# Expert tokens past 128 as plain float32 blocks of 32 over four column quarters, gate-weighted results added to the residual rows in DRAM

## The chip, the cores and the metric

The kernel runs on one core of one Trainium2 chip. The metric is the device time of one execution in microseconds (us). Before the change three runs took 3171.59, 3177.5 and 3178.11 us, so the median is 3177.5 us. One more execution, of 3167.94 us, was recorded by the hardware profiler; every row below is from that one.

## The reference, cut to what matters

A block takes 2048 tokens of width 1024. A token mixer (not touched, but for the order of one loop) makes a residual `x`. A router then picks two of 32 experts for each token, with a weight each, and the experts' results are added to the residual:

```
f = modulate(rms_norm(x, norm_ffn_w), m[3], m[4])            # [2048, 1024]
g = softmax(f @ rg_w + rg_b);  top group, its probability p
e = (f @ re_w + re_b) of that group's 8 experts;  top 2
weight = p * softmax(top 2)                                   # 2 per token
for each of the 4096 assignments (token t, expert k):
    out = (silu(f[t] @ w1[k]) * (f[t] @ w3[k])) @ w2[k]       # 1024 -> 512 -> 1024
y[t] = sum over its two assignments of weight * out
x = x + m[5] * y
return rms_norm(x, final_norm_w)
```

All is float32. On the inputs used, 15 of the 32 experts get more than 128 assignments, 4 of these more than 160, and none more than 192.

## The kernel before, in words

**Three stages matter.** (1) The project and route stage makes `x1` and `f` for 16 tiles of 128 tokens, stores them in DRAM (`X1`, `FR`), computes 36 router logits a token (`logits`, line 678, then a transpose back, `placed`) and from them a table of row numbers for every expert. (2) The expert stage is a loop over 32 experts. (3) The tail reads the experts' results back from `YB` in DRAM, two rows a token, multiplies them by the weights (ScalarE, line 1046), adds them (lines 1048 to 1051), multiplies by `m5` (line 1054), adds the residual (line 1055), and normalises (lines 1057, 1186, 1187, 1062), tile by tile.

**Precision.** A float32 product is done as three fast products (`mm3`, lines 1356 to 1358) of a rounded part `hi` and a remainder `lo`. ScalarE makes `hi` of a 128x1024 block of weights (line 1212), VectorE or GpSimd makes `lo` (line 1213). Twelve such blocks of 512 KB make one expert.

**One expert.** GpSimd gathers 128 rows of `FR` by an indirect DMA (line 848, tile `xg128`), and, when the expert has more than 128 rows, up to 64 more (`xg64`). TensorE transposes them (line 865). `up` makes 2x512 columns and `down` 1024. The *main* rows take 72 products of 128x512 columns, 48 up and 24 down. The *rest* rows sit behind a branch (`tc.If(big > 128)`, line 873): their `hi` and `lo` are laid side by side as 128 columns, so two products per weight block do (line 880): 32 up and 16 down, 48 for each expert that has a rest. A scatter by GpSimd (line 917) writes the results to the assignment's row of `YB`.

**Order.** Every engine has one queue and works it in order. The code is written with one expert's `down` after the next expert's `up`, a scheduler then fixes the order of each queue, and pools of buffers (`mraw` 9, `mhi` and `mlo` 15 each) decide how far the loads of weights, on SyncE's queue, run ahead. The gather of an expert waits until the transposes of the expert before it have freed `xg128`. A branch costs each engine that takes part in it a compare and a jump, also where it isn't taken.

**In the mixer**, `d_states` (line 314) multiplies with 64 rows of the array at a time; `g` is the outer loop, the chunk `c`, whose parity picks the lower or the upper 64 rows, the inner one. Elsewhere there (lines 429, 434) a product uses 64 columns of the array and the heads take the two column halves in turn.

Of the kernel before, what the change touches and what calls it, by code (L numbers as in the profile page):

```python
# [181 lines left out]
def ssm(G, tc, dtr, XR, ZT, XC, XB, cumD, ecumD, elD, SBd, YT):  # L182
# [4 lines left out]
    with tc.tile_pool(reuse_waits="tile", name="sst", bufs=1) as st:  # L187
# [86 lines left out]
        with tc.tile_pool(reuse_waits="tile", name="sw", bufs=1) as wp, tc.tile_pool(reuse_waits="tile", name="ssp", bufs=2) as sp:  # L274
# [292 lines left out]
RAW, PARTS = 9, 15  # L567
AHEAD = 6
# [3 lines left out]
def ffn(tc, G, A, out, bcast, rsqrt, split, mm3, MT, MR, X1, FR, YB, mid):  # L572
# [7 lines left out]
    wt = [rp.tile([128, N], F32, name=f"wt{k}") for k in range(2)]  # L580
# [5 lines left out]
    asg = rp.tile([128, NBK], I32, name="asg")  # L586
    idx = rp.tile([128, NBK], I32, name="idx")
    ovt = rp.tile([128, 2 * OVB + 1], I32, name="ovt")
    ovf = rp.tile([128, OVB], F32, name="ovf")

    def assign(dst_a, dst_r, v, t):
# [3 lines left out]
        nc.vector.tensor_copy(dst_a, v)  # L595
        nc.vector.tensor_scalar(t, v, float(T), float(-T), op0=OP.is_ge, op1=OP.mult)
        return nc.vector.tensor_add(dst_r, v, t)
# [4 lines left out]
    with tc.tile_pool(reuse_waits="tile", name="wo", bufs=1, side="right") as wop, \  # L602
# [19 lines left out]
        rb = wop.tile([36, 1], F32, name="rb")  # L622
        nc.sync.dma_start(rb, A["rb"])
# [20 lines left out]
        def project(i, *between):  # L644
# [13 lines left out]
            nc.sync.dma_start(X1[i], x1)  # L658
# [4 lines left out]
        def turned(i, x1, f, ss_, lg):  # L663
# [8 lines left out]
            nc.sync.dma_start(FR[i * 128:(i + 1) * 128], f)  # L672
            return fT, lg

        def logits(fT, lg):
            pl = psum("sc")
            for k in range(8):
                nc.tensor.matmul(pl[0:36, 0:128], rw[:, k], fT[:, k], start=k == 0, stop=k == 7)
            lt = tp.tile([36, 128], F32, name="lt", bufs=2)
            nc.vector.tensor_scalar(lt, pl[0:36, 0:128], rb, None, op0=OP.add)  # L680
            return lt, lg

        def placed(lt, lg):
            pl = psum("sc")
            nc.tensor.transpose(pl[:, 0:36], lt, G.ident[0:36, 0:36])
            nc.vector.tensor_copy(lg, pl[:, 0:36])

        def route(p0, i0, M, lg):
# [77 lines left out]
            nc.vector.tensor_mul(wt[0][:, i0:i0 + M], pg, v1)  # L766
            nc.vector.tensor_mul(wt[1][:, i0:i0 + M], wt[0][:, i0:i0 + M], v2)
# [7 lines left out]
        for p, i in enumerate(order):  # L775
# [6 lines left out]
            def second(p=p):  # L782
                tiles[p] = logits(*tiles[p])
# [3 lines left out]
            at.setdefault(2 * p + 4, []).insert(0, lambda p=p: placed(*tiles[p]))  # L787
            if last:
                at[2 * p + 4].append(lambda g=(p0, i0, M, lg): route(*g))
            tiles[p] = i, *project(i, lambda: do(2 * p), lambda: do(2 * p + 1))  # L790
        for h in range(2 * N, 2 * N + 3):
# [4 lines left out]
        listed = assign(asg, idx, tab.rearrange("p s e -> p (s e)"), at)  # L796
# [11 lines left out]
    def unit(src, q=nc.sync, eng=nc.vector):  # L808
# [5 lines left out]
        return hi, lo  # L814

    class InTurn:

        def __init__(self, src):
            self.src, self.at, self.parts = src, None, None

        def __getitem__(self, u):
            if u != self.at:
                raw = ovp.tile([128, 1024], F32, name="oraw")
                nc.sync.dma_start(raw, self.src(u))
                hi = wp.tile([128, 1024], F32R, name="ohi", tag="xq")
                lo = wr.tile([128, 1024], F32R, name="olo", tag="xg64")
                split(raw, hi, lo)
                self.at, self.parts = u, (hi, lo)
# [3 lines left out]
    hf = [psum(f"hf{i}") for i in range(2)]  # L832
    for p in hf:
        nc.vector.memset(p, 0.0)

    xgs = [wr.tile([128, D], F32, name=f"xg{r}") for r in (128, 64)]
    for x in xgs:
        nc.gpsimd.memset(x, 0.0)
    xgs[1] = xgs[1][0:64]


    ENGINES = [mybir.EngineType.PE, mybir.EngineType.Pool]
    outs = []

    def gather(idx_ap, half, guard):
        xg = xgs[half]
        with guard():
            nc.gpsimd.indirect_dma_start(out=xg, out_offset=None, in_=FR,  # L848
                                         in_offset=bass.IndirectOffsetOnAxis(ap=idx_ap, axis=0),
                                         bounds_check=T - 1, oob_is_err=False)  # L850
        return xg

    def parts(src, n, half, name):

        r = 64 if half else 128
        if half:
            q = wp.tile([128, n, 128], F32R, name=name + "q")
            hi, lo = q[:, :, 0:64], q[:, :, 64:128]
        else:
            hi, lo = (wp.tile([128, n, 128], F32R, name=name + c) for c in "hl")  # L860
        for c in range(0, n, 512 // r):
# [4 lines left out]
            v = pt[:, :m * r].rearrange("p (k t) -> p k t", t=r)  # L866
            nc.scalar.copy(hi[:, c:c + m], v)
            nc.vector.tensor_sub(lo[:, c:c + m], v, hi[:, c:c + m].bitcast(F32))
        return [q] if half else [hi, lo]

    def products(ps, x, ws, n, guard):

        with guard():
            for p, w in zip(ps, ws):
                if len(x) == 2:
                    mm3(p, lambda k: (x[0][:, k], x[1][:, k]), w, range(n))
                else:
                    for k in range(n):
                        for i, wk in enumerate(w(k)):
                            nc.tensor.matmul(p, x[0][:, k], wk, start=k + i == 0, stop=k == n - 1 and i == 1)  # L880

    def whole(dst, p):

        nc.scalar.copy(dst, p[64:128])
        nc.vector.tensor_add(dst, dst, p[0:64])  # L885

    def up(x, w1, w3, guard):
        half = len(x) == 1
        pa = hf if half else [psum("mm"), psum("mm")]
        wv = lambda w: lambda k: tuple(t[:, (k % 2) * 512:(k % 2) * 512 + 512] for t in w[k // 2])  # L890
        products(pa, x, [wv(w1), wv(w3)], 8, guard)
        h = wp.tile([64 if half else 128, FF], F32, name=f"mh{int(half)}")
        if half:
            g = wp.tile([64, FF], F32, name="mg")
            whole(h, pa[0])
            whole(g, pa[1])
            nc.scalar.activation(h, h, AF.Silu)
            nc.vector.tensor_mul(h, h, g)
        else:
            nc.scalar.activation(h, pa[0], AF.Silu)  # L900
            nc.vector.tensor_mul(h, h, pa[1])
        return h

    def down(h, w2, guard, dst):
        half = len(h) == 1
        y = wp.tile([128, D], F32, name=f"my{int(half)}")[0:64 if half else 128]
        py = hf if half else [psum("sc"), psum("sc")]
        wv = lambda w, o: lambda k: tuple(t[:, o:o + 512] for t in w[k])
        products(py, h, [wv(w, 512 * c) for c, w in enumerate(w2)], 4, guard)
        if half:  # L910
            whole(y[:, 0:512], py[0])
            whole(y[:, 512:1024], py[1])
        else:
            nc.scalar.copy(y[:, 0:512], py[0])
            nc.vector.tensor_copy(y[:, 512:1024], py[1])
        with (guard if half else nullcontext)():
            d = nc.gpsimd.indirect_dma_start(out=YB, out_offset=bass.IndirectOffsetOnAxis(ap=dst, axis=0), in_=y,
                                             in_offset=None, bounds_check=2 * T - 1, oob_is_err=False)
        for o in outs:
            tc.declare_no_dep(d.ins, o.ins, reason="rows of other assignments")  # L920
        outs.append(d)

    def fetch(e_, b, guard):
        s = b * NE + e_
        return parts(gather(idx[0:64 if b else 128, s:s + 1], b, guard), 8, b, "x")
# [7 lines left out]
    def beyond():  # L933
# [5 lines left out]
        le = ovp.tile([128, OVB, 32], BF, name="le")  # L939
# [22 lines left out]


    x = [fetch(0, 0, nullcontext), fetch(0, 1, nullcontext)]
# [3 lines left out]
    big = nc.values_load(cnti[0:1, 0:1], engines=ENGINES, min_val=0, max_val=CAP)  # L968
    nguard = lambda big=big: tc.If(big > 128)
    for e_ in range(NE + 1):  # L970
        if e_ < NE:
            guard = nguard
            if e_ + 1 < NE:
                big = nc.values_load(cnti[0:1, e_ + 1:e_ + 2], engines=ENGINES, min_val=0, max_val=CAP)
                nguard = lambda big=big: tc.If(big > 128)
            h = [up(x[0], *w13, nullcontext), None]
            q = nc.sync if e_ else nc.gpsimd
        if last:
            t1 = parts(last[1], 4, 1, "h")
        if e_ < NE:  # L980
            h[1] = up(x[1], *w13, guard)
            if e_ + 1 < NE:
                x[0] = fetch(e_ + 1, 0, nullcontext)
                w13 = in_weights(e_ + 1, q)
            w2 = [unit(A["e2"][e_][:, u], q, eng=nc.gpsimd if u % 2 else nc.vector) for u in range(4)]
        if last:
            down(last[0], [last[2]] * 2, nullcontext, asg[:, e_ - 1:e_])
            down(t1, [last[2]] * 2, last[3], asg[0:64, NE + e_ - 1:NE + e_])
        if e_ < NE:
            last = parts(h[0], 4, 0, "h"), h[1], w2, guard  # L990
            if e_ + 1 < NE:
                x[1] = fetch(e_ + 1, 1, nguard)
# [4 lines left out]
    m5, fn, *e = [rp.tile([128, D], F32, name="mraw") for _ in range(RAW)]  # L997
# [582 lines left out]
```

## Time and profile before

| what | us |
|---|---|
| median of three runs | 3177.5 |
| the profiled execution | 3167.94 |
| its span | 3166.2 |
| expert stage, from 2246 to 3049 | 803 |
| tail, from the last product on TensorE at 3049 to the end | 117 |

Over the whole span TensorE (PE) is busy 2876.7 us (91%), VectorE (DVE) 1893.4 us (60%), ScalarE (ACT) 1243.8 us (39%) and GpSimd (POOL) 853.5 us (27%). HBM was read for 501.47 MB and written for 129.27 MB. TensorE's granted clock is a mean of 0.956 of its full level. A busy share is to be read by stage: in the expert stage TensorE hardly pauses, in the tail it does nothing.

### The profile page before, as it was taken

How to read it: one execution, taken by the hardware profiler on the slowest of the kernel's cores; microseconds unless marked ns; L12 is line 12 of the kernel's file. 1: busy time of each engine (PE TensorE's matmuls, PEld its weight loads, DVE VectorE, ACT ScalarE, POOL GpSimd, SP SyncE). 2: the span in 40 equal slices, each digit the busy share in tenths (PEclk: the TensorE clock that was granted, in tenths of full speed). 3: DMA queues.
4: the chain of work that ended last, by engine and by line, in shares of the span. 5: the costliest groups of instructions: out<-in, count | busy, mean ns of one | idle time of the engine just before them, and what ended most of it. 6: DMA issues, size and time to landing. Idle time of an engine off the chain costs nothing. (4 is left out here: it accounts for less than half of the span.)

```text
span 3166.2 us, 40956 instructions
## 1 busy us (share of the span) xinstructions
PE 2876.7 (91%) x14805; PEld 2291.8 (72%) x14805; DVE 1893.4 (60%) x2957; ACT 1243.8 (39%) x1754; POOL 853.5 (27%) x589
## 2 busy tenths in 40 slices
PE   7998999999877999899999999999699999999950
PEld 4887887777655677677777777877577887778740
DVE  4524125878775587333334334566888767786758
ACT  5411132322345032232113122222677667675744
POOL 3300010000014021013334333000446445444445
PEclk8999999999978899999999999999799999999975
DMA  7635244423128486765336335432788878887884
GB/s 303 233 122 194 86 159 155 140 84 106 51 82 272 123 225 208 244 233 199 130 120 216 126 120 163 143 133 107 276 310 308 283 271 322 299 302 271 283 327 172
DMA packets 241878, 625.50 MB, mean 198 GB/s; under 512 B 27832, under 2 KB 75608, under 8 KB 237944
## 3 DMA queue, kind: packets, MB, share of 16 engines
q1 hardware_dynamic: 208784, 513.34, 47.0%
q0 software_dynamic: 32880, 109.38, 10.2%
q8 instruction: 126, 2.06, 0.3%
q14 instruction: 88, 0.72, 0.1%
HBM read 501.47 MB, written 129.27 MB: 199 GB/s over the span
## 5 line engine op out<-in xcount | busy, mean ns | idle before, releaser
L1212 ACT CAST mhi<-mraw 128x1024 fp32r<-128x1024 f32 x384 | 387.3, 1051 | 12.8 <-DMA mraw<-e 12.4
L1213 DVE TENSOR_TENSOR mlo<-mraw,mhi 128x1024 fp32r<-128x1024 f32 x318 | 378.2, 1242 | 2.8 <-ACT mhi L1212 2.2
L1356 PE MATMUL ps_mm<-hb1h,wlo 128*128 128x512 f32 x800 | 320.6, 401 | 3.1 <-DVE wlo L1213 3.1
L1507 ACT ACTIVATE ev<-ps_mm 128x512 f32<-128x512 f32 x128 | 76.3, 598 | 617.4 <-PE ps_mm L1358 508.6
L1358 PE MATMUL ps_mm<-hb1h,whi 128*128 128x512 f32 x800 | 318.7, 398 | 0.0
L1357 PE MATMUL ps_mm<-hb1l,whi 128*128 128x512 f32 x800 | 318.3, 398 | 0.0
L1213 DVE TENSOR_TENSOR wlo<-wraw,whi 128x1024 fp32r<-128x1024 f32 x164 | 217.9, 1337 | 149.2 <-ACT whi L1212 149.0
L1356 PE MATMUL ps_mm<-hb0h,wlo 128*128 128x512 f32 x672 | 270.1, 402 | 16.5 <-DVE wlo L1213 12.9
L1357 PE MATMUL ps_mm<-hb0l,whi 128*128 128x512 f32 x672 | 270.1, 402 | 0.0
L1358 PE MATMUL ps_mm<-hb0h,whi 128*128 128x512 f32 x672 | 268.6, 400 | 0.0
L1557 POOL TENSOR_TENSOR macc<-macc,ev 128x512 f32<-128x512 f32 x96 | 167.0, 1740 | 306.8 <-DVE ev L1556 303.8
L1213 POOL TENSOR_TENSOR mlo<-mraw,mhi 128x1024 fp32r<-128x1024 f32 x66 | 212.9, 3241 | 133.9 <-ACT mhi L1212 124.2
L1212 ACT CAST whi<-wraw 128x1024 fp32r<-128x1024 f32 x176 | 182.1, 1045 | 154.4 <-PE ps_mm L1358 65.8
L1556 DVE TENSOR_TENSOR ev<-ev,ps_tr 128x512 f32<-128x512 f32 x96 | 65.7, 686 | 248.5 <-PE ps_tr L1358 244.8
L1356 PE MATMUL ps_mm<-mhi,xl 128*128 128x512 f32 x512 | 204.7, 400 | 0.1
L1358 PE MATMUL ps_mm<-mhi,xh 128*128 128x512 f32 x512 | 200.9, 392 | 0.3
L848 POOL DMA_INDIRECT xg<-d_FR,idx x48 | 129.4, 2696 | 264.8 <-PE ps_tr L865 196.7
L1357 PE MATMUL ps_mm<-mlo,xh 128*128 128x512 f32 x512 | 200.5, 392 | 0.3
L1356 PEld LDWEIGHTS ps_mm<-hb1h,wlo 128*128 128x128 f32 x800 | 151.7, 190 | 38.0 <-DVE wlo L1213 3.5
L1358 PEld LDWEIGHTS ps_mm<-hb1h,whi 128*128 128x128 f32 x800 | 151.6, 190 | 34.3 <-issue 2.8
L1357 PEld LDWEIGHTS ps_mm<-hb1l,whi 128*128 128x128 f32 x800 | 151.8, 190 | 31.9 <-issue 1.6
L1356 PEld LDWEIGHTS ps_mm<-hb0h,wlo 128*128 128x128 f32 x672 | 128.1, 191 | 46.5 <-DVE wlo L1213 14.9
(605 smaller groups left out, 6486.0 us busy)
## 6 DMA issues: line engine op xcount, KB each, us to landing
mraw<-e SPq DMA_DIRECT2D x372, 512.0 KB
wraw<-wg SPq DMA_DIRECT2D x80, 512.0 KB
wraw<-wt SPq DMA_DIRECT2D x40, 512.0 KB
aw<-adaw SPq DMA_DIRECT2D x64, 256.0 KB
d_GS<-ev SPq DMA_DIRECT2D x64, 256.0 KB
ev<-d_GS POOLq DMA_DIRECT2D x64, 256.0 KB, 4.6
yk<-d_YB SPq DMA_DIRECT2D x32, 512.0 KB
wraw<-wg POOLq DMA_DIRECT2D x24, 512.0 KB, 4.2
```

The lines of the kernel that those rows point to most:

```text
L848: nc.gpsimd.indirect_dma_start(out=xg, out_offset=None, in_=FR, in_offset=bass.IndirectOffsetOnAxis(ap=idx_ap, axis=0), bounds_check=T - 1 ...
L1212: nc.scalar.copy(hi, raw)
L1213: eng.tensor_sub(lo, raw, hi.bitcast(F32))
L1356: nc.tensor.matmul(ps, wl, xh, start=start and n == 0, stop=False)
L1357: nc.tensor.matmul(ps, wh, xl, start=False, stop=False)
L1358: nc.tensor.matmul(ps, wh, xh, start=False, stop=stop and n == len(ks) - 1)
L1507: nc.scalar.activation(g, ps, AF.Sigmoid)
L1556: nc.vector.tensor_mul(g, g, ps)
L1557: nc.gpsimd.tensor_add(acc, acc, g)
```

## The change

- **Rest rows.** They are no longer split. The transposed rows stay plain float32 (`plain`, tile `xq`), 32 at a time are the stationary operand, and the raw weights `mraw` are the moving operand, 256 columns a product. `quarters` puts four such products side by side, one for each quarter of 32 columns of the array. A block of 32 rows is behind its own branch: block 0 if the expert has more than 128 rows, block 1 if it has more than 160. A block is 32 products up and 16 down. With these inputs there are 15 + 4 = 19 blocks.
- **Weights at the gate.** `FR` gets a 1025th column with the assignment's weight and is stored twice, once for each of a token's two assignments. The gather brings the weight along, and it is multiplied in where `silu` meets the other half (lines 904 and 944); `m5` is multiplied in behind `down` (lines 921 and 952).
- **Results.** The scatter (line 908) adds to the rows of `X1` in DRAM; unused rows of a block go to 256 spare rows. Scatters to the same rows are ordered one after the other: the rest of an expert waits until its predecessor's main scatter has landed.
- **Tail.** It reads only `X1`, and normalises.
- **Buffers.** `mraw` 9 to 16, `mhi` and `mlo` 15 to 12 each. Raw blocks are held until the rest products have read them.
- **Router and mixer.** The logits are made with tokens on the rows (36 columns moving) and need no transpose back. In `d_states` the chunk is the outer loop.

```diff
-                for g, c in product(range(2), cs):
+                for c, g in product(cs, range(2)):
...
-RAW, PARTS = 9, 15
+RAW, PARTS = 16, 12
...
-            nc.sync.dma_start(FR[i * 128:(i + 1) * 128], f)
+            for k in range(2):
+                nc.sync.dma_start(FR[k * T + i * 128:k * T + (i + 1) * 128, 0:D], f)
...
-                nc.tensor.matmul(pl[0:36, 0:128], rw[:, k], fT[:, k], start=k == 0, stop=k == 7)
+                nc.tensor.matmul(pl[:, 0:36], fT[:, k], rw[:, k], start=k == 0, stop=k == 7)
...
+            for k in range(2):
+                nc.sync.dma_start(FR[k * T:k * T + T].rearrange("(i p) w -> p i w", p=128)[:, i0:i0 + M, D:D + 1],
+                                  wt[:, i0:i0 + M, k:k + 1])
...
+    def added(y, dst, out, no_dep=()):
+        d = nc.gpsimd.indirect_dma_start(out=out, out_offset=bass.IndirectOffsetOnAxis(ap=dst, axis=0), in_=y,
+                                         in_offset=None, compute_op=OP.add)
...
+    def quarters(p, n, guard, x, ws):
+
+        for j in range(2):
+            with guard(j):
+                for k, g in product(range(n), range(4)):
+                    nc.tensor.matmul(p[g * 32:g * 32 + 32, j * 256:j * 256 + 256], x(k, j), ws(k, g),
+                                     start=k == 0, stop=k == n - 1)
+
+    def up_rest(xw, w1, w3, guard):
+
+        w = [w1, w3]
+        quarters(hu, 8, guard, lambda k, j: xw[0][:, k, j * 32:j * 32 + 32],
+                 lambda k, g: w[g // 2][k // 2][2][:, (k % 2) * 512 + (g % 2) * 256:][:, 0:256])
...
+    def down_rest(h, w2, guard, e_):
+
+        quarters(hd, 4, guard, lambda k, j: h[:, j * 2 + k % 2, (k // 2) * 32:(k // 2) * 32 + 32],
+                 lambda k, g: w2[k][2][:, g * 256:g * 256 + 256])
+        y = wp.tile([128, 2, 256], F32, name="my1")
+        nc.vector.tensor_mul(y, hd.rearrange("p (j n) -> p j n", j=2), m5x.unsqueeze(1).to_broadcast([128, 2, 256]))
+        d = []
+        for j in range(2):
+            with guard(j):
+                d.append(added(y[:, j], sct4[:, e_, j:j + 1], X1.rearrange("r (g n) -> (r g) n", g=4), d))
+        return d
...
-    R = [(*rows(i), i) for i in range(AHEAD)]
-    for i in range(19):
-        if i + AHEAD < 16:
-            R.append((*rows(i + AHEAD), i + AHEAD))
-        if i < 16:
-            scaled(*R[i])
-        if 2 <= i < 18:
-            R[i - 2] += added(*R[i - 2]),
-        if i >= 3:
-            normed(*R[i - 3])
+    for i, t in enumerate(x1s):
+        nc.sync.dma_start(t, X1[i * 128:(i + 1) * 128])
+    for i, t in enumerate(x1s):
+        sq = wr.tile([128, D], F32, name="yk", tag=("mhi", "mlo")[i % 2], bufs=PARTS)
+        ss_ = wp.tile([128, 2], F32, name="ss3", bufs=4)
+        nc.scalar.activation(sq, t, AF.Square, accum_out=ss_[:, 0:1])
+        rsqrt(ss_[:, 1:2], ss_[:, 0:1], D, 1)
+        nc.vector.scalar_tensor_tensor(t, t, ss_[:, 1:2], fn, op0=OP.mult, op1=OP.mult)
+        nc.sync.dma_start(out[0][i * 128:(i + 1) * 128], t)
```

GpSimd's queue over one expert in the middle of the loop, before: `xg` is the gathers' tile, `mlo` the remainder of two weight blocks, `d_YB` the results in DRAM; L916 and L847 are the branches for the rest.

```order
541 L848 DMA xg_16987<-d_FR,idx 128x1024
...
545 L847 COMPARE_AND_BRANCH
546 L848 DMA xg_16988<-d_FR,idx 64x1024
...
550 L1213 TENSOR_TENSOR mlo<-mraw,mhi 128x1024 x2
551 L917 DMA d_YB<-my_21849,asg 4096x1024
552 L916 COMPARE_AND_BRANCH
553 L917 DMA d_YB<-my_21881,asg 4096x1024
...
559 L848 DMA xg_16987<-d_FR,idx 128x1024
```

The same after: `d_X_97` are the residual rows, `sct` and `sct4` the row numbers, and L955 the branches for the two rest blocks.

```order
654 L850 DMA xg_16950<-d_FR,idx 128x1025
...
657 L850 DMA xg_16951<-d_FR,idx 64x1025
...
665 L908 DMA d_X_97<-my_21968,sct 2304x1024
666 L1215 TENSOR_TENSOR mlo<-mraw,mhi 128x1024
...
671 L1215 TENSOR_TENSOR mlo<-mraw,mhi 128x1024
672 L955 COMPARE_AND_BRANCH
673 L908 DMA d_X_97<-my_22056,sct_17006 9216x256
...
677 L955 COMPARE_AND_BRANCH
678 L908 DMA d_X_97<-my_22056,sct_17006 9216x256
...
682 L850 DMA xg_16950<-d_FR,idx 128x1025
```

The main scatter now stands ahead of the two splits, the rest scatters behind them, and each gather stands behind the rest scatters, as it stood behind the scatters before.

TensorE's queue before, at the start of one expert's rest products: `xq` holds the rest rows, L873 is the branch.

```order
8675 L1358 MATMUL ps_mm<-mhi,xh 128x512
8676 L1356 MATMUL ps_mm<-mhi,xl 128x512
8677 L873 COMPARE_AND_BRANCH
8678 L880 MATMUL ps_hf_16983<-mhi,xq 128x512
8679 L880 MATMUL ps_hf_16983<-mlo,xq 128x512
```

After, the two blocks of another expert in the middle of the loop, each behind its own branch, L928.

```order
10016 L1360 MATMUL ps_mm<-mhi,xh 128x512
10017 L1358 MATMUL ps_mm<-mhi,xl 128x512
10018 L928 COMPARE_AND_BRANCH
10019 L930 MATMUL ps_hf_16946<-mraw,xq 32x256 x32
10020 L928 UNCONDITIONAL_BRANCH x2
10021 L928 COMPARE_AND_BRANCH
10022 L930 MATMUL ps_hf_16946<-mraw,xq 32x256 x32
10023 L928 UNCONDITIONAL_BRANCH x2
10024 L1359 MATMUL ps_mm<-mlo,xh 128x512
```

The rest products stay among the main products of the same expert; there are two branches where there was one.

VectorE's queue at the end of the tail, before: `ss` is one tile's sum of squares, `mraw` holds residual rows and `m5`, `yk` the results read back.

```order
2558 L1054 TENSOR_TENSOR yk_26833<-yk_26833,mraw 128x1024
2559 L1062 SCALAR_TENSOR_TENSOR mraw<-mraw,ss_26927 128x1024
2560 L1055 TENSOR_TENSOR mraw<-mraw,yk_26833 128x1024
2561 L1054 TENSOR_TENSOR yk_26849<-yk_26849,mraw 128x1024
2562 L1186 TENSOR_SCALAR ss_26935<-ss_26935 128x1
2563 L1055 TENSOR_TENSOR mraw<-mraw,yk_26849 128x1024
2564 L1062 SCALAR_TENSOR_TENSOR mraw<-mraw,ss_26935 128x1024
```

After:

```order
2489 L1189 TENSOR_SCALAR ss_28202<-ss_28202 128x1
2490 L1077 SCALAR_TENSOR_TENSOR mraw<-mraw,ss_28202 128x1024
2491 L1189 TENSOR_SCALAR ss_28209<-ss_28209 128x1
2492 L1077 SCALAR_TENSOR_TENSOR mraw<-mraw,ss_28209 128x1024
2493 L1189 TENSOR_SCALAR ss_28216<-ss_28216 128x1
```

Two instructions a tile are left, and each tile's pair is finished before the next one's begins.

## Rows read from the trace of the kernel before

**Rows 1.** Busy time by engine, a stretch of the expert stage, and the project stage

```profile
core 0: us, PE busy (x) PEld busy (x) DVE busy (x) ACT busy (x) POOL busy (x), PEclk, DMA share, GB/s
2340.00:2440.00 100.00, 98.42 (x477) 77.93 (x475) 85.47 (x104) 76.03 (x103) 61.84 (x22) 1.00 0.90 326
...
1905.00:2225.00 320.00, 312.63 (x1560) 247.78 (x1559) 188.58 (x488) 80.87 (x149) 40.27 (x40) 0.99 0.40 138
```

**Rows 2.** TensorE's timeline inside one rest: start, duration, line, tiles

```profile
2573.62 0.39 PE L880 MATMUL ps_hf<-mlo,xq 128*128 128x512 f32 x1
...
2576.79 0.40 PE L880 MATMUL ps_hf<-mlo,xq 128*128 128x512 f32 x1
```

**Rows 3.** The rest products alone over the expert stage, columns as far as ACT

```profile
2246.00:3049.00 803.00, 169.03 (x720) 134.94 (x720) 81.28 (x126) 71.65 (x126) 0.99 0.84 297
```

**Rows 4.** Timeline of plain float32 products, 256 moving columns, whole array

```profile
19.56 3.62 PE L1253 MATMUL ps_mm<-ha1h,s 128*2 128x256 f32 x16
23.11 0.28 PE L1261 MATMUL ps_sc<-c_kid,mr 2*128 2x2 f32 x2
```

**Rows 5.** Timeline of products by halves of the array, in the mixer

```profile
1107.44 0.64 PE L434 MATMUL ps_tr<-ec,Sf 128*64 128x64 f32 x16
1108.01 0.66 PE L319 MATMUL ps_sc<-xw,xb 64*64 64x128 f32 x8
1108.60 0.66 PE L429 MATMUL ps_tr<-PT,xb 128*64 128x128 f32 x8
```

**Rows 6.** Weight loads of line 434 there: duration in ns, minimum, median, maximum

```profile
L434 PEld LDWEIGHTS ps_tr<-ec,Sf x16: 137/138/138, 1107.3 to 1107.8; 128*64 128x64 f32 x16
```

**Rows 7.** Line 873, the rest's branch, in the expert stage

```profile
L873 PEldq COMPARE_BRANCH  x90: 65/169/357, 2304.4 to 3040.4; - x90
```

**Rows 8.** Gathers in the expert stage, and what their issue waited for

```profile
  PE ps_tr L865: 193.5, 35
...
DMA to landing us min/median/max: 4.2/8.1/12.9
```

**Rows 9.** Scatters in the expert stage

```profile
DMA to landing us min/median/max: 3.3/3.5/3.7
```

**Rows 10.** The tail, windows: its middle, its end, and its first loads

```profile
3063.00:3158.00 95.00, 0.00 (x0) 0.00 (x0) 86.77 (x72) 49.88 (x63) 54.67 (x32) 0.50 0.63 242
3158.00:3167.00 9.00, 0.00 (x0) 0.00 (x0) 0.00 (x0) 0.00 (x0) 0.00 (x0) 0.50 0.15 59
3060.00:3090.00 30.00, 0.00 (x0) 0.00 (x0) 23.64 (x18) 19.36 (x22) 17.45 (x9) 0.50 1.03 412
```

**Rows 11.** Chain of waits into the tail and at its end: start, duration

```profile
3052.67 3.73 DMA d_YB<-my,asg
...
3058.23 5.18 DMA yk<-d_YB
...
3152.45 0.17 DVE ss L1186
...
3152.75 1.41 POOL ss L1187
3154.18 1.28 DVE mraw L1062
```

**Rows 12.** Around the last product, and a tile's sum of squares, timeline

```profile
3048.79 0.39 PE L1358 MATMUL ps_sc<-mhi,hh 128*128 128x512 f32 x1
...
3069.80 1.06 ACT L1057 ACTIVATE yk<-xk 128x1024 f32<-128x1024 f32 x1 [3.92 <-DVE xk L1055]
```

**Rows 13.** Timeline of one tile's router logits

```profile
2000.73 1.94 PE L678 MATMUL ps_sc<-hb0l,rw 128*36 128x128 f32 x16
2002.60 0.50 PE L1356 MATMUL ps_mm<-y00h,wlo 128*128 128x512 f32 x1
```

**Rows 14.** Products of line 319 and of the logits, whole run

```profile
L319 PE MATMUL ps_sc<-xw,xb x280: 269/269/473, 956.0 to 1225.9; 64*64 64x128 f32 x140
...
L678 PE MATMUL ps_sc<-hb0l,rw x256: 272/273/421, 2000.7 to 2222.9; 128*36 128x128 f32 x128
```

More of the change, by code (lines that the diff above doesn't have):

```diff
@@ L849, in gather, with turned_into @@
                                          in_offset=bass.IndirectOffsetOnAxis(ap=idx_ap, axis=0),
-                                         bounds_check=T - 1, oob_is_err=False)
+                                         bounds_check=2 * T - 1, oob_is_err=False)
         return xg
[L853 to L860, printed above, removed]
+    def turned_into(put, src, r, n, w=128):
         for c in range(0, n, 512 // r):
@@ L865, in parts @@
                 nc.tensor.transpose(pt[:, k * r:(k + 1) * r], src[:, (c + k) * 128:(c + k + 1) * 128], G.ident[:r, :r])
[L866 to L901, printed above, removed]
-        return h
@@ L904, in down @@
[L904 to L921, printed above, removed]
@@ L923, in fetch, with parts, put @@
-    def fetch(e_, b, guard):
-        s = b * NE + e_
-        return parts(gather(idx[0:64 if b else 128, s:s + 1], b, guard), 8, b, "x")
+            put(slice(c, c + m), pt[:, :m * r].rearrange("p (k t) -> p k t", t=r))
+    def parts(src, n, name):
+        hi, lo = (wp.tile([128, n, 128], F32R, name=name + c) for c in "hl")
+        def put(c, v):
+            nc.scalar.copy(hi[:, c], v)
+            nc.vector.tensor_sub(lo[:, c], v, hi[:, c].bitcast(F32))
+        turned_into(put, src, 128, n)
+        return hi, lo
@@ new lines, in plain, with turn, turn_rest @@
+    def plain(src, n, name):
+        t = wp.tile([128, n, 64], F32, name=name)
+        turned_into(lambda c, v: nc.scalar.copy(t[:, c], v), src, 64, n)
+        return t
+    def turn(xg):
+        p = parts(xg, 8, "x")
+        w = wp.tile([128, 1], F32, name="w0", bufs=2)
+        nc.scalar.copy(w, xg[:, D:D + 1])
+        return p, w
+    def turn_rest(xg):
+        p = plain(xg, 8, "xq")
+        w = wp.tile([64, 2], F32, name="w1", bufs=2)
+        for j, h in product(range(2), range(2)):
+            nc.scalar.copy(w[h * 32:h * 32 + 32, j:j + 1], xg[j * 32:j * 32 + 32, D:D + 1])
+        return p, w
@@ new lines, in down @@
+    def down(h, w2, dst, rest=()):
+        y = wp.tile([128, D], F32, name="my0")
+        py = [psum("sc"), psum("sc")]
+        for c, (p, ws) in enumerate(zip(py, w2)):
+            o = slice(512 * c, 512 * c + 512)
+            mm3(p, lambda k: (h[0][:, k], h[1][:, k]), lambda k: tuple(t[:, o] for t in ws[k][:2]), range(4))
+            nc.vector.tensor_mul(y[:, o], p, m5[:, o])
+        added(y, dst, X1, rest)
+    def quarters(p, n, guard, x, ws):
[4 more added lines that the diff above has]
+                                     start=k == 0, stop=k == n - 1)
@@ L961, in beyond, with fetch @@
         nc.vector.scalar_tensor_tensor(ovf, bj, 128.0, ej, op0=OP.mult, op1=OP.add)
-    x = [fetch(0, 0, nullcontext), fetch(0, 1, nullcontext)]
+    def fetch(e_, guard):
+        xs = gather(idx[:, e_:e_ + 1], 0, nullcontext), gather(idx[0:64, NE + e_:NE + e_ + 1], 1, guard)
+        return lambda: (turn(xs[0]), turn_rest(xs[1]))
+    x = fetch(0, lambda: nullcontext())()
+    sct4 = wr.tile([128, NE, 2], I32, name="sct4")
+    for g, j in product(range(4), range(2)):
+        nc.gpsimd.tensor_scalar(sct4[g * 32:g * 32 + 32, :, j], sct[j * 32:j * 32 + 32, NE:], 4.0, float(g), op0=OP.mult, op1=OP.add)
     with tc.issue_after(listed.ins):
@@ L973, in ffn @@
             if e_ + 1 < NE:
-                big = nc.values_load(cnti[0:1, e_ + 1:e_ + 2], engines=ENGINES, min_val=0, max_val=CAP)
-                nguard = lambda big=big: tc.If(big > 128)
-            h = [up(x[0], *w13, nullcontext), None]
+                nguard = over(load(e_ + 1))
+            up_rest(x[1], *w13, guard)
+            h1 = gate_rest(x[1])
+            h = up(x[0], *w13)
+            t1 = plain(h1, 4, "hq")
             q = nc.sync if e_ else nc.gpsimd
+            if e_ + 1 < NE:
+                x = fetch(e_ + 1, lambda: nguard(0))()
+                w13 = in_weights(e_ + 1, q)
@@ L989, in ffn @@
[L989 to L992, printed above, removed]
+            rest = down_rest(t1, w2, guard, e_)
+            last = parts(h, 4, "h"), w2, rest
             if e_ == 4:
                 beyond()
-    m5, fn, *e = [rp.tile([128, D], F32, name="mraw") for _ in range(RAW)]
-    x1s = [wr.tile([128, D], F32, name="xk", tag=("mhi", "mlo")[i % 2], bufs=PARTS) for i in range(16 - len(e))] + e
@@ L1006, in ffn @@
+    otiles = x1s.pop(), *(wr.tile([128, 1024], F32R, name="o" + n, tag=n, bufs=PARTS) for n in ("mhi", "mlo"))
     with tc.issue_after(fetched.ins):
@@ L1053, in added @@
-    def added(y0, y1, x1, i):
-        nc.vector.tensor_mul(y0, y0, m5)
-        nc.vector.tensor_add(x1, x1, y0)
+        w1, w3 = (InTurn(lambda u, n=n: f2(n, u), otiles) for n in ("e1", "e3"))
+        w2 = [InTurn(lambda u: dy("e2")[:, u], otiles) for _ in range(2)]
+        h = up(turn(gather(ix, 0, nullcontext)), w1, w3)
+        down(parts(h, 4, "h"), w2, ixs)
+    for i, t in enumerate(x1s):
+        nc.sync.dma_start(t, X1[i * 128:(i + 1) * 128])
+    for i, t in enumerate(x1s):
+        sq = wr.tile([128, D], F32, name="yk", tag=("mhi", "mlo")[i % 2], bufs=PARTS)
```

152 lines of the change are left out of this document (68 added, 84 removed).

## Prediction

> **What bounds the kernel now.** I read the busy time by stretch first. In the expert stage TensorE works 98.42 of 100 us at a granted clock of 1.00, the upper of its two levels, while VectorE has 85, ScalarE 76 and GpSimd 62, and the DMA engines are at a share of 0.90 [rows 1]. The reader is to see that every other engine has room there, the transfers least. So the 803 us of this stage are a sum of TensorE's instructions, and the rest products are 169.03 us of them by busy time (720 records, 15 experts with 48 products each) [rows 3]. The project stage is TensorE's too, 312.63 of 320 us [rows 1]. Then the tail: from the last product at 3048.79 [rows 12] to the end of the span, 117 us, TensorE has nothing, and VectorE is busy 86.77 of the 95 us in the middle [rows 10]. The chain of waits shows how the tail starts (a scatter lands, 3.73, then the first load, 5.18) and ends (sum of squares, GpSimd's power, VectorE's multiply) [rows 11].
>
> **Rest products removed.** Two records of a rest 14 apart start 3.17 us apart, so one product costs 0.2264 us [rows 2], and 720 cost 163.0 us.
>
> **Rest products added.** 19 blocks of 48 products. A plain float32 product leaves two records, and over the whole array one with 256 moving columns steps by (23.11 - 19.56)/16 = 0.222 us [rows 4]. That is 96 records a block, 21.3 us if each takes the whole array's time, 10.7 if two run at once and 5.33 if four do. The trace has no product by quarters. It has products by column halves: 16 records with 64 moving columns start and end within 0.57 us, and 8 with 128 within 0.49 us before the next line starts, about 0.036 and 0.061 each [rows 5], where 128 columns on one column group step by (2002.60 - 2000.73)/16 = 0.117 [rows 13]. So two halves run at once, at twice the rate, with different moving data. I take four at once, the nearest in kind, 19 x 5.33 = 101 us, and keep 10.7 and 21.3 as the other end.
>
> The weight loads are what speaks against this: each quarter needs its own, on the same 128 rows. The loads there take 0.137 us each [rows 6], sixteen of them within the 0.57 us above, so they lie beside the products. The Trainium skill says in "TensorE: Matmul & The Clock Gate", Part 3, that a weight load overlaps running products only when the row group differs, which is not so for column quarters. This case's rows for halves disagree with that rule. If it held for quarters, one load in each group of four would be bare: 24 x 0.137 = 3.3 us a block, 62 us in all; that is a rival below.
>
> **Branches.** Each expert has seven on TensorE instead of four, 96 more in all. One compare takes 0.065 to 0.357 us, median 0.169 [rows 7]: 16 us, between 6 and 34.
>
> **Other waits in the expert stage.** Per expert, ScalarE and VectorE lose the copies of the rest's halves and gain little, so they get freer. GpSimd is the one to look at, since a gather now stands behind the rest scatters. Before, the gather's issue waited 193.5 us in 35 cases for TensorE to free its tile [rows 8], so it is issued as soon as the transposes are done and needed one expert later, about 20 us; it lands after 4.2 to 12.9 us. After, what stands ahead of it (main scatter, two splits, rest scatters) belongs to the expert before and ends at about the time when the tile comes free, so a delay up to some 7 us costs nothing. The transfers: an expert without a rest moves 12 x 0.524 MB of weights, 0.52 MB in the gather and 0.52 in the scatter, 7.3 MB, and a scatter that adds reads its rows as well, 7.9 MB. The stretch in rows 1 had 326 GB/s at a share of 0.90, that is 362 at a full one, so such an expert needs 20.3 to 21.7 us, and TensorE about the same: 72 main products at 0.2264 are 16.3, with transposes and branches near 20. Before, experts with a rest gave the loads time to catch up; they now take 5 us more than the others and not 11. I put 20 us for waits of this kind and for the tighter order behind 12 instead of 15 split buffers, between 0 and 45. The stage: -163 + 101 + 16 + 20 = -26 us.
>
> **The tail.** What goes: two reads, two weightings and three additions a tile. What is left is serial: VectorE's queue has a tile's mean, then its multiply, then the next tile's, and the multiply waits for GpSimd. From the chain one such turn is 3152.45 to 3154.18, 1.73, and a multiply of 1.28, 3.0 us [rows 11]; sixteen are 48. Ahead of it: one multiply and one scatter, 2.5 us (before, four copies and two scatters took 3.5 to 3052.67), landing 3.73, 1.8 to the first load's start, which can't be issued ahead any more, its landing 5.18 [rows 11], and one sum of squares, 1.06 [rows 12]. Behind it the last store: from 3158 on no engine is busy for the 8.2 us to the end [rows 10]. The loads, 8.4 MB at 412 GB/s [rows 10], take 20 us and hide. Sum 2.5 + 3.7 + 1.8 + 5.2 + 1.1 + 48 + 8.2 = 71 (rounded up) instead of 117: -46 us. No row shows how long an adding scatter takes to land; between the plain one's 3.5 and twice that [rows 9], which is +4 here. If the power and the multiply overlapped across tiles, the tail would be up to 25 us shorter; the order in the queue rules this out.
>
> **Ahead of the expert stage.** Line 319's 280 records [rows 14] run from alternating row halves, 0.074 each (8 in 0.59) [rows 5]; with consecutive products in the same half I take 0.117, +12 us at most where TensorE is full. The logits' 256 records [rows 14] go from 128 to 36 moving columns: 0.117 each now, not below 36/128 of it, so between 0 and -21 us, and I take -15, with the transposes back. The first gather now waits for the weights' column, stored in 4-byte pieces: one landing more, 4 us [rows 8]. FR's second copy lies in a stage with a DMA share of 0.40 [rows 1]. Sum about 0, between -12 and +15.
>
> **Sum.** 3167.9 - 26 - 46 + 0 = 3096 for an execution like the profiled one. That one lies 9.6 us under the median of the runs, so 3106.
>
> **Rivals.**
> - *Quarters run two at a time, or not at once at all.* For it: rows show halves only. Against: halves overlap without loss. Decides from 10.7 us a block: 19 x 5.33 = +101 us, 3207, slower than before; with no overlap 19 x 16 = +304, 3410.
> - *Weight loads of the same rows don't hide* (the skill's rule above): +62 us, 3168, a little faster still.
> - *The adding scatters are slow.* Main and rest scatters form one chain over the experts, and GpSimd stands still for a landing in it, with the next gather behind. An expert with a rest lasts about 26 us, so two landings and some 5 us of issues fit while one landing is under 10 us; the trace has 3.5 for plain ones [rows 9]. At 15 us it would be 35 - 26 = 9 us for each of 15 experts and some for the others, about +100, 3206, slower.
> - *The transfers become the bound.* At 21.7 us and more for experts without a rest, and less time to catch up in the others: +40 us, 3146.
>
> **How the numbers follow.** Forecast as summed 0.58 (own range 3065 to 3145); exposed loads 0.10; two at a time 0.10 and none 0.03; slow adding scatters 0.08; transfers 0.11. What a measurement of this kernel can tell from no change is about 0.2%, 6 us. Faster holds the forecast, the transfers and most of the exposed loads, with some taken off for costs that add up: 0.73. Slower holds two at a time, none, the scatters and a little: 0.22. Same 0.05. The low end 3060 has waits and branches at their low bounds and the front at -12 (3106 - 20 - 10 - 12 = 3064); the high end 3210 takes in two at a time and the scatters.
>
> **What would show it.** In the profile after: rest products, line 930, with four records starting within some 20 ns and 5.3 us for a block's 96 records (10.7 would show the first rival); TensorE still over 95% busy between 2340 and 2940, and idle ahead of its transposes of `xg` if the gathers are late, or ahead of `hi` and `lo` if the transfers bound; an adding scatter's landing near 3.5 to 7 us; a tail of about 71 us with VectorE, GpSimd and VectorE in turn. The forecast is wrong if the stage isn't shorter than 803 us by 10 at least, or the tail isn't under 80.

## The result, and the profile after

The changed kernel takes 3200.72 us (median of nine runs), beside 3169.71 us for the kernel before on the same chips. The ratio is 1.0094, with a 95% interval from 1.0066 to 1.0121: slower by about 1%, where 3106 and faster were forecast. The profiled execution has a span of 3190.7 us, 24.5 longer than before.

Two parts explain these 24.5 us. The tail, from the last product to the end, fell from 117 to 54 us. The expert stage, from the first transposes of gathered rows to the last product, rose from 802 to 903 us. (It began at 2246.6 before and at 2233.9 here; in the profiled executions of this document it begins anywhere between 2226 and 2250, so these 13 us need not be a gain of the change.) First the busy time by stretch of the changed kernel, to be held against [rows 1] (columns as there):

```profile
core 0: us, PE busy (x) PEld busy (x) DVE busy (x) ACT busy (x) POOL busy (x), PEclk, DMA share, GB/s
2246.00:3137.00 891.00, 778.33 (x4865) 565.63 (x4863) 608.12 (x622) 505.31 (x755) 342.01 (x169) 0.94 0.77 263
...
2900.00:3000.00 100.00, 84.62 (x672) 58.58 (x670) 47.11 (x51) 44.88 (x67) 28.11 (x14) 0.91 0.59 193
```

TensorE pauses for 113 of the 891 us in the first row, where it paused for 13 of 803 before. No other engine is near full, and the transfers have fallen from a share of 0.84 to 0.77, so none of them has become the bound by its amount of work. The granted clock has fallen with TensorE's pauses, to 0.91 in the last row. Something in the middle makes one engine wait for another. The rest products themselves (line 930) went as forecast, on TensorE's timeline:

```profile
2537.63 1.93 PE L930 MATMUL ps_hf<-mraw,hq 128*32 128x256 f32 x32
2539.74 0.47 PE L1358 MATMUL ps_mm<-mhi,xl 128*128 128x512 f32 x1 [0.18 <-PEq L928]
```

Those 32 records are 16 products in four quarters, 8 groups of four that start 0.216 us apart; 1.93 runs to the end of the last record, which is itself 0.38 long. All 1824 records of the 19 blocks are busy for 105.59 us, where the 720 of before were for 169.03 [rows 3]. So the stage, 100 us longer, lost some 160 us elsewhere. The waits of the whole stage, grouped (who waited, for whom, us in total, times, longest):

```profile
POOL d_X L908 <- DVE my L921: 230.6, 26, 13.3
DVE mlo L1215 <- ACT mhi L1214: 187.9, 80, 9.7
POOL mlo L1215 <- ACT mhi L1214: 130.5, 26, 18.9
ACT w L892 <- DMA xg<-d_FR,idx: 95.8, 16, 10.2
ACT w L884 <- DMA xg<-d_FR,idx: 66.4, 17, 6.8
POOL xg L850 <- PE ps_tr L861: 54.9, 17, 15.6
...
PE ps_mm L1358 <- ACT mhi L1214: 29.5, 10, 5.9
...
PE ps_tr L861 <- DVE xl L870: 21.2, 11, 4.0
```

Read backwards: of TensorE's waits, 110 us in all, the longest are for `mhi`, the rounded weights that ScalarE makes, and for `xl`, a remainder that VectorE makes; VectorE and GpSimd wait for `mhi` too; and ScalarE, which makes it, waits 162.2 us in 33 cases for the gather `xg`, in front of a copy `w`. ScalarE's timeline shows one such case:

```profile
2526.61 1.06 ACT L1214 CAST mhi<-mraw 128x1024 fp32r<-128x1024 f32 x1
2527.56 0.60 ACT L877 COPY xq<-ps_tr 128x512 f32<-128x512 f32 x1
2533.57 0.19 ACT L892 COPY w<-xg 32x1 f32<-32x1 f32 x1 [5.41 <-DMA xg<-d_FR,idx]
2533.67 1.04 ACT L1214 CAST mhi<-mraw 128x1024 fp32r<-128x1024 f32 x1
```

and GpSimd's the gathers that it waits for, issued when TensorE had freed the tile:

```profile
2525.61 1.06 POOL L850 DMA_INDIRECT xg<-d_FR,idx  x1 [0.38 <-PE ps_tr L861]
2527.66 0.97 POOL L850 DMA_INDIRECT xg<-d_FR,idx  x1 [0.98 <-PE ps_tr L861]
```

The copy takes 0.19 us. It takes the next expert's weight out of the 1025th column, and in ScalarE's queue it stands right behind `xq` of the expert at hand. Here ScalarE comes to it at 2528.16, 0.5 us after the issue of the gather that it reads, the one of 64 rows. Over the 33 waits ScalarE comes a median of 1.3 us after that issue, in nine of them before it, and a gather lands 7.8 us after its issue (median; before 8.1 [rows 8]). In the queue of the changed kernel, where w_23234 and w_23247 are one expert's weights:

```
1106 L877 COPY xq<-ps_tr 128x512
1107 L892 COPY w_23247<-xg_16951 32x1 x2
1108 L1214 CAST mhi<-mraw 128x1024
1109 L884 COPY w_23234<-xg_16950 128x1
1110 L892 COPY w_23247<-xg_16951 32x1 x2
1111 L1214 CAST mhi<-mraw 128x1024
```

What is queued behind it are the casts that everything else needs. TensorE notices a few us later, here at the transposes at 2553.41, which waited 3.76 us for a result buffer that VectorE hadn't emptied yet, since its remainders came late. ScalarE's wait is not all of that: VectorE had waited 5.51 us for `mhi`, but one of its remainders also took 5.92 us, from 2540.91, where the others took 1.22, while GpSimd made two of its own.

The tail after, VectorE's and GpSimd's turn on the chain of waits, against [rows 11]:

```profile
3174.11 0.16 DVE ss L1189
...
3174.41 0.56 POOL ss L1190
...
3176.19 0.16 DVE ss L1189
```

One turn is 2.08 us.

### The profile page after: what moved, and what is told of

Its sections match the earlier page's. It is cut to its first block, busy times and chain, and to the rows that moved or that the text cites. A ratio compares the mean times of both kernels' runs of the same rounds, so it can differ in the third digit from the quotient of the medians.

```text
span 3190.7 us, 43392 instructions
## 1 busy us (share of the span) xinstructions
PE 2864.6 (90%) x15893; PEld 2233.7 (70%) x15893; DVE 1823.1 (57%) x2806; ACT 1154.0 (36%) x1722; POOL 763.2 (24%) x586
## 5 line engine op out<-in xcount | busy, mean ns | idle before, releaser
L1215 DVE TENSOR_TENSOR mlo<-mraw,mhi 128x1024 fp32r<-128x1024 f32 x318 | 445.5, 1420 | 189.0 <-ACT mhi L1214 187.9
L1358 PE MATMUL ps_mm<-mhi,xl 128*128 128x512 f32 x512 | 213.9, 418 | 38.0 <-ACT mhi L1214 29.5
L1359 PE MATMUL ps_mm<-mlo,xh 128*128 128x512 f32 x512 | 212.1, 414 | 17.0 <-DVE mlo L1215 7.1
L1215 POOL TENSOR_TENSOR mlo<-mraw,mhi 128x1024 fp32r<-128x1024 f32 x66 | 189.1, 2928 | 144.5 <-ACT mhi L1214 130.5
L1360 PE MATMUL ps_mm<-mhi,xh 128*128 128x512 f32 x512 | 208.8, 408 | 5.5 <-PEq L928 5.5
L908 POOL DMA_INDIRECT d_X<-my,sct x51 | 105.5, 2068 | 309.8 <-DVE my L921 230.6
```

Of the source, the lines that this page charges most:

```text
L908: d = nc.gpsimd.indirect_dma_start(out=out, out_offset=bass.IndirectOffsetOnAxis(ap=dst, axis=0), in_=y, in_offset=None, compute_op=OP.add)
L1215: eng.tensor_sub(lo, raw, hi.bitcast(F32))
L1358: nc.tensor.matmul(ps, wl, xh, start=start and n == 0, stop=False)
L1359: nc.tensor.matmul(ps, wh, xl, start=False, stop=False)
L1360: nc.tensor.matmul(ps, wh, xh, start=False, stop=stop and n == len(ks) - 1)
```

## The experiments

Three theories were set against each other: (A) ScalarE's copies wait for the gather, and this delays the casts; (B) the adding scatters are slow and hold GpSimd and the gathers; (C) fewer split buffers and raw blocks held longer keep the loads back. For (B) there was a row: adding scatters landed 9.1 us after their issue (median), where plain ones took 3.5 [rows 9].

```profile
DMA to landing us min/median/max: 4.8/9.1/12.4
```

These two medians can't be held against each other. The 3.5 is of two scatters alone, issued at 3020.7 and 3052.7, when the DMA engines were at a share of 0.43 and 0.55 and not 0.90; the view has a landing for only 2 of the 47 before, and for 10 of the 51 after. By the completion signals in the traces, 41 of the 47 plain scatters can be followed, and they land after 3.3 to 10.7 us, median 7.6; of the adding ones 44 can, median 8.1.

**The copies behind their own expert's casts.**

```diff
-        nc.scalar.copy(w, xg[:, D:D + 1])
+        with tc.issue_after(casts["x"].ins):
+            nc.scalar.copy(w, xg[:, D:D + 1])
...
+          with tc.issue_after(casts["xq"].ins):
             nc.scalar.copy(w[h * 32:h * 32 + 32, j:j + 1], xg[j * 32:j * 32 + 32, D:D + 1])
```

> Edit: the copies of an expert's gate weights on ScalarE are queued behind the cast of the same expert's transposed rows, so they no longer stand one expert early, ahead of the casts of weights. Nothing else changes. Theory A (the copies wait for the next gather's landing, 162 us in 33 waits on ScalarE, and the casts, the remainders and TensorE's products behind them are late): the waits for xg on ScalarE fall under 10 us, TensorE's busy share between 2300 and 3000 rises from 0.88 to over 0.95, the time falls by 70 to 95 us from 3200.7, to 3105 to 3130. Theory B (the adding scatters, which land in 9.1 us and not 3.5, hold GpSimd and the gathers): 3185 or more. Theory C (12 instead of 15 split buffers, raw blocks held longer): 3185 or more.

Measured: 3101.54 us, ratio to before 0.9751 (0.9734 to 0.9767); the waits for `xg` are gone from ScalarE's list, and TensorE is busy 0.95 of the time between 2300 and 3000. ScalarE's timeline in the same place:

```profile
2522.66 0.59 ACT L873 CAST xh<-ps_tr 128x512 fp32r<-128x512 f32 x1
2523.14 0.20 ACT L893 COPY w<-xg 128x1 f32<-128x1 f32 x1
2523.23 1.06 ACT L1224 CAST mhi<-mraw 128x1024 fp32r<-128x1024 f32 x1
2524.18 0.60 ACT L884 COPY xq<-ps_tr 128x512 f32<-128x512 f32 x1
2524.66 0.79 ACT L902 COPY w<-xg 32x1 f32<-32x1 f32 x4
2525.47 1.99 ACT L1224 CAST mhi<-mraw 128x1024 fp32r<-128x1024 f32 x2
```

The same five copies, 1 us of work, wait for nothing. This is theory A, at 99 us a little over its range (109 by the two ratios to before, since the chips differed).

**Scatters that write instead of adding.**

```diff
-                                         in_offset=None, compute_op=OP.add)
+                                         in_offset=None)
```

> Edit: the scatters write instead of adding; left out is the sum of a token's two results and its residual. Theory A: the scatters land sooner, the waits of ScalarE for xg stay (150 us or more in all), the time stays within 12 us of the changed kernel's 3200.7. Theory B: landing near 3.5 us, 3105 to 3140. Theory C: within 12 us of 3200.7.

Measured: 3182.99 us, ratio to before 1.0015 (0.9997 to 1.0034), 18 us less than the changed kernel (25 by the ratios). That is more than A allowed and far less than B needs. The scatters landed after 2.4 to 10.9 us, median 6.5, and the gathers after 6.5 instead of 7.8. ScalarE's waits for `xg` stayed, 88.3 and 62.7 us. What a sooner landing is worth while ScalarE waits for it is part of those 18 us; the rest is below.

**Weights from a constant tile.**

```diff
-        nc.scalar.copy(w, xg[:, D:D + 1])
+        nc.scalar.copy(w, wone)
...
-            nc.scalar.copy(w[h * 32:h * 32 + 32, j:j + 1], xg[j * 32:j * 32 + 32, D:D + 1])
+            nc.scalar.copy(w[h * 32:h * 32 + 32, j:j + 1], wone[j * 32:j * 32 + 32])
```

> Edit: the gate weights are copied from a constant tile instead of the gathered rows; left out are the true weights. The copies stay on ScalarE, in number and size. Theory A: the wait is gone, the time is that of the run with the copies queued behind the casts, within 10 us (3100 to 3130), so it is the wait and not the copies' own time. Theory B and C: 3185 or more.

Measured: 3112.86 us, ratio 0.9792 (0.9776 to 0.9809). The copies are still there and nothing in them can wait for a gather. So it is the wait, not the copies, and (C), which this edit leaves as it was, isn't the cause of these 88 us. The 11 us to the first run are a little more than expected; in the profile 6.6 us of them are two waits of TensorE for GpSimd's remainders, which the first run has not.

**The mixer's loop back.** The first edit, and:

```diff
-                for c, g in product(cs, range(2)):
+                for g, c in product(range(2), cs):
```

> Edit: as the run with the weight copies behind the casts, and the mixer's loop of line 317 back with g outside and the chunk inside. Theory A and the prediction's step for line 319 (up to 12 us from 280 records that no longer run two at a time, partly hidden): 0 to 12 us less than that run; the windows from 950 to 1230 shorter by as much. If row halves don't matter: the same within 5 us.

Measured: 3102.72 us, 0.9747 (0.9725 to 0.9769). No difference that the runs can tell. TensorE is busy 260.05 of 280 us from 950 to 1230 against 258.84, so the order of the products of line 319 gains nothing back.

**A buffer of its own for the fifth expert's code.** The first edit, and:

```diff
-        le = wp.tile([128, OVB, 32], BF, name="le", tag="mh1")
+        le = ovp.tile([128, OVB, 32], BF, name="le")
```

> Edit, on top of the run with the weight copies behind the casts: the table of the fifth expert's extra code (tile le) gets a buffer of its own instead of sharing that of mh1, the rest's half result. In that run expert 5 took 34.0 us from transpose to transpose, before 23.5, and ScalarE's silu of the rest waited 7.46 us for VectorE's last step of that code. If the shared buffer is the cause: expert 5 takes 22 to 24 us and the time falls by 8 to 12 us, to 3090 to 3094. If the code's own time on VectorE is the cause: under 4 us.

Measured: 3104.88 us, 0.9775 (0.9742 to 0.9807), not less. Yet the local effect is there: expert 5 takes 21.4 us and not 34.0. The schedule of the later experts changed as well, and TensorE there has a wait that the first run has not (from 2400 to 3010):

```profile
PE ps_sc L1369 <- POOL mlo L1225: 11.4, 4, 3.8
```

What was gained at expert 5 was lost at experts 26 to 29.

**One register for each engine.** The first edit, and branches taken by the one engine that has work in them:

```diff
-    load = lambda e_: nc.values_load(cnti[0:1, e_:e_ + 1], engines=ENGINES, min_val=0, max_val=CAP)
-    over = lambda big: lambda j: tc.If(big > 128 + 32 * j)
+    load = lambda e_: [nc.values_load(cnti[0:1, e_:e_ + 1], engines=[g], min_val=0, max_val=CAP) for g in ENGINES]
+    over = lambda bigs: [lambda j, b=b: tc.If(b > 128 + 32 * j) for b in bigs]
...
```

> Edit, on top of the run with the weight copies behind the casts: the counts are loaded into one register for TensorE and one for GpSimd, so a branch around a gather or scatter is taken by GpSimd alone and one around products by TensorE alone: 4 branches an expert on TensorE instead of 7, 2 to 3 on GpSimd instead of 7. The prediction's step of 0.169 us a branch on TensorE: 95 fewer, 16 us less, 3086. If branches without products behind them cost TensorE nothing because its queue runs ahead (no wait for L965 stands in the trace): within 5 us of 3101.5.

Measured: 3101.08 us, 0.9763 (0.9722 to 0.9804). A branch without products behind it costs TensorE nothing that these runs can tell, where 16 us were expected. Those with products remain: in the first run 55 waits of 0.18 to 1.3 us, 26.2 us together.

**Scatters that write, with the wait gone.** The first edit and the second one together.

> Edit, on top of the run with the weight copies behind the casts: the scatters write instead of adding; left out is the sum of a token's two results and its residual. The same edit on the changed kernel gave 18 us. If the adding scatters cost by holding GpSimd and the gathers: 10 to 20 us here as well. If those 18 us were the gathers' sooner landing, for which ScalarE's copies waited: under 6 us, of which 3 at the last scatter (landing 5.94 there, 3.73 for a plain one).

Measured: 3090.25 us, 0.9727 (0.9693 to 0.9760), against 0.9751 (0.9734 to 0.9767). The medians differ by 11 us, the intervals overlap: adding costs this kernel 0 to some 15 us, and the runs can't tell more. In the profiled executions the stage took 799 us against 804, and the scatters landed after 6.7 us (median) against 8.0.

**One quarter after the other.** The first edit, and:

```diff
-                for k, g in product(range(n), range(4)):
+                for g, k in product(range(4), range(n)):
```

> Edit, on top of the run with the weight copies behind the casts: the rest products take one column quarter after the other (quarter outside, weight block inside) instead of all four in turn; the number of products and their operands are the same. If the quarters' overlap is what makes a block 5.2 us: a block's 96 records step by 0.216 us each, 20.7 us a block, 19 x 15.5 = 295 us more, 3395. If the products cost the same in any order: 3101.

Measured: 3284.78 us, 1.0350 (1.0314 to 1.0386): 183 us more, 9.6 a block. The same 64 records of one up block, first with the quarters in turn, then one after the other:

```profile
2321.41 3.66 PE L940 MATMUL ps_hf<-mraw,xq 128*32 128x256 f32 x64
```

```profile
2313.34 11.50 PE L940 MATMUL ps_hf<-mraw,xq 128*32 128x256 f32 x64
```

The gain hangs on the order of issue, as expected, but neighbours still overlap where one quarter hands over to the next, so the loss is 183 and not 295.

**The fifth expert's code in the last expert's turn; expert 1's weights from SyncE's queue; both.** The first edit, and one or both of:

```diff
-            if e_ == 4:
+            if e_ == NE - 1:
...
-            q = nc.sync if e_ else nc.gpsimd
+            q = nc.sync
```

> Edit, on top of the run with the weight copies behind the casts: the code that shares mh1's buffer runs in the last expert's turn instead of the fifth's. If expert 5's 34.0 us come from that buffer: expert 5 takes 22 to 24 us and, other than with a buffer of its own, the order of the later experts stays as it was: 9 to 13 us less, 3089 to 3092. If the code's work comes back ahead of the tail: within 3 us of 3101.5.

> Edit, on top of the run with the weight copies behind the casts: the weights of expert 1 are loaded from SyncE's queue instead of GpSimd's, so that the gather of expert 2 no longer stands behind those loads, which wait for buffers (TensorE waited 5.65 us for that gather). If that is the cause of the slow start: experts 1 and 2 together take 5 us less and the time falls by 4 to 8 us, to 3094 to 3098. If transfers bound the start: within 3 us of 3101.5.

> Both edits of the two other runs of this call, as the best version that the experiments point to: the sum of the two, 3082 to 3090, if the two stretches are independent.

Measured: 3110.37 (ratio 0.9784, 0.9752 to 0.9816), 3112.59 (0.9787, 0.9754 to 0.9820) and 3106.06 us (0.9759, 0.9721 to 0.9797). None is faster than the first run, though the intervals overlap. (The profiled execution of the first of the three took 3089.84 us, the shortest of its five; it owes that to a stage that began 15 us sooner, and the stage itself took 809 us against 804.) Again each edit did its own: expert 5 took 21.5 us in the first, experts 1 and 2 took 41.3 instead of 49.9 us in the second. And again it was lost after expert 23: in the run with both, between 2860 and 3012,

```profile
PE ps_sc L1369 <- POOL mlo L1225: 11.6, 4, 3.8
```

The version to keep is thus the changed kernel with its copies queued behind their own casts.

## Why the prediction was wrong

**The step that failed** is the one on the other waits of the expert stage: "ScalarE and VectorE lose the copies of the rest's halves and gain little, so they get freer. GpSimd is the one to look at". ScalarE did get freer in work, 505 us busy in the stage instead of 561. But of the five copies that it gained, 0.19 us each, the first must wait for a transfer, and I had read the new order of GpSimd's, TensorE's and VectorE's queues and not ScalarE's. The forecast put the copies at nothing. It names what waits for the gather on TensorE, whose slack of one expert, 20 us, is real; the new reader of the same tile on ScalarE has a slack of about 1.3 us against a landing of 7.8. What the runs showed in its place are 162 us of waits on ScalarE, worth 99 us of the kernel's time. None of the four rivals holds them. By the forecast's own sign, a stage that is shorter than 803 us by 10 at least, it fails too: 903. With that wait taken out the time is 3101.5; forecast were 3106.

That closeness is luck. It hides two errors of opposite sign, seen in the run with the copies behind the casts (span 3100.0):

- *Rest products removed and added:* right. Four quarters at once, 216 ns for a group of four records, 105.59 us busy for 19 blocks. The rule of the Trainium skill that was weighed ("TensorE: Matmul & The Clock Gate", Part 3, a weight load overlaps only products of another row group) is not what this trace shows for column quarters: each group has four weight loads of 0.106 to 0.110 us on the same 128 rows, twice the step when laid end to end, and steps by 0.216 all the same.
- *Branches:* 16 us came from a wrong count. Those without products cost nothing that shows; those with products made TensorE wait in 55 cases, 26.2 us, against 1.0 us before. The 41 cases among the `up` products are 20.6 us of it:

```profile
PE ps_mm L1368 <- PEq L938: 6.9, 14, 0.8
PE ps_mm L1369 <- PEq L938: 6.9, 15, 0.8
PE ps_mm L1370 <- PEq L938: 6.8, 12, 1.3
```

- *The stage, -26:* not there. From the first transposes of expert 0 to the last product it is 803.5 us, before 802.2. The rest products took 63 us less, as summed, but TensorE's pauses rose from 12 to 50 us, 25 of these by the branches, and the 2304 main products took 20 us more from start to start, part of it at a lower clock, for which the sum had no term. From expert 10 to the start of 31 it took 507.4 us where before took 535.0, 28 less, and that is where the term was meant to come from. But experts 0 to 9 took 252.8 instead of 219.9, 33 more. About 11 of these are expert 5, 34.0 us instead of 23.5: the code for experts past 192 now shares its buffer with the rest's half result, and ScalarE waits 7.46 us for VectorE to be done with it. About 12 are experts 1 and 2, 49.9 instead of 38.2, of which the run with the loads on SyncE's queue took back 8.6: a gather stands behind loads that wait. Both were shown by runs, and both were given back elsewhere by other orders, so what the stage could reach stays open.
- *The tail, -46:* it was -63. The order of the turn was right, its size was not: a turn is 2.08 us and not 3.0, sixteen are 33 and not 48, because GpSimd's power took 0.55 us and not the 1.41 of [rows 11]. In that row an instruction of VectorE on two whole tiles (line 1055) was running beside the power, and the new tail has none (see the last section).
- *Ahead of the stage, 0:* about right; the first transposes started at 2246.6 before and between 2226 and 2250, median 2241, in the profiled runs after.
- *Adding scatters:* landing was priced between 3.5 and 7 us, but the 3.5 of [rows 9] was of two scatters at the end of the stage, and the plain ones before took 7.6 (median). In the repaired kernel adding ones took 8.0 and plain ones 6.7. Adding is worth 0 to some 15 us. (That rival's sum was off as well: 9 us for each of 15 experts are 135, not about 100.)
- *Transfers:* no bound that shows; the DMA engines are at a share of 0.86 in the repaired stage, and ScalarE waited for raw expert weights for 16.5 us in all.

How much of the stage's 100 us is the granted clock and how much the pauses themselves can be read from the trace. The clock was 0.99 over the stage before, 0.94 in the changed kernel and 0.97 in the repaired one. Of the 2304 main products, 171 step by about 0.43 us and not 0.23 in the changed kernel, 155 of them at the lower level, 0.50; before there were 19 such steps, in the repaired kernel 50. That is about 36 us against before, and 8 in the repaired kernel. TensorE's pauses are the larger part: 114 us against 12.

## What to carry to other kernels

A tiny instruction in a busy engine's queue costs the wait that it brings, not its length: for each new reader of a transferred tile, ask on which queue it stands, what stands behind it, and how long before it the transfer was issued. Read the order of every engine that gains an instruction, also of the one that gains 1 us of work. And a scheduler answers a local edit with another order far away, so judge an edit by its stretch and by the total both.

## What the runs showed of the hardware that was not expected

- Four float32 products on four column quarters, each with its own moving rows and its own load of the stationary operand, take the time of one: starts 6 to 7 ns apart, 216 ns a group, where one alone over the whole array stepped by 222 [rows 4]. One quarter after the other, 64 records take 11.50 us instead of 3.66; only the last four records of a quarter still overlap the first four of the next.
- GpSimd's power on 128 numbers takes 0.55 us in the changed tail. In the one before, it took 1.40 to 1.48 us in the 15 of 16 cases where VectorE was in the middle of a 1.2 us product or sum of two tiles (lines 1054, 1055), and ended some 0.4 us behind that; the sixteenth had no VectorE instruction beside it and took 0.55. VectorE's remainders show the same from the other side: their median is 1.22 us, and each one over 1.5 us runs beside a remainder that GpSimd makes. There are 7 of these before (18 us), 37 in the changed kernel (109 us) and 32 in the repaired one (92 us). No run changed this by itself, so what it costs the stage is not shown.

```profile
L1190 POOL TENSOR_TENSOR ss<-ss,mhalf 128x1 f32<-128x1 f32 x16 | 8.8, 549 | 34.1 <-DVE ss L1189 34.1
```

- Under the load of the expert stage an indirect scatter of up to 128 rows landed after 8.1 and 8.0 us (median, changed and repaired kernel) where it adds to the residual rows, after 6.5 and 6.7 where it writes to them, and after 7.6 before, to rows of its own in `YB`. The 3.3 and 3.7 us of the two in [rows 9] were measured with the DMA engines at about half their share.
